# A trunk layer in split fp32: one pool's buffers change the start of all large tiles, and the third gate pass prepares its weights in another way

## Chip, core and metric

The kernel runs on one core of a Trainium2 chip. The metric is the device time of one execution in microseconds; before the change it is 1064.31 us (median of 3 runs, 1064.09 to 1064.84). Less is better.

## What is computed

One layer of a trunk on 256 tokens of width 2048: a gated linear attention mixer (4 heads, keys of 256, values of 512, chunks of 64 tokens), then a squared-ReLU MLP with 8192 hidden units, each behind an RMS norm and with a residual, and a last RMS norm.

```
proj = h @ w_in                                  # h = rmsnorm(x): q, k, v, r, g_low
log_a = log_sigmoid(g_low @ w_gate_up + b_gate) / 16
...                                              # per chunk: state = decay * state + k^T v; o = q state
o = rmsnorm(o) * o_norm
x = x + (o * silu(r)) @ w_out
a = relu(rmsnorm(x) @ w_up)
x = x + (a * a) @ w_down
```

## The kernel before

All products are in fp32 by parts. A matrix is split in a high part (a CAST on ScalarE, L1199 in the later stages) and a low part (raw minus high, on VectorE, L1205), and a product is three matmuls: high x high, high x low, low x high. A matmul has a stationary operand of 128x128 and a moving one of 128x256; 9014 of them of several stages follow each other without a break: the value pass with the gate's low rank (L149), keys and queries (L181), the scores, the second half of the values (L149), four gate passes named r, c = 0 to 3 (L669; the attention itself, L149, lies among the first), four passes of the output projection named o (L669), and then the MLP, in which up pieces (L1241) and down pieces (L1361) alternate, 48 and 42 matmuls; a tail of the down product (L149) closes it. In L1241 and L181 the weights are the stationary operand and the rows (tiles h, or x: names hh and hl, xh and xl, with h and l for high and low part) move; in L149, L669 and L1361 the rows are stationary (xh, xl, oth, otl, acts) and the weights move.

Some of the gate, o and down pieces ("summed doubles") use a scheme with 7 block products in place of 8. They need sums of weight blocks: one block is added onto another in the raw tile (rawu), then three sums are built (tile sums: L519 twice, L520), and the sums are split in turn into the tile sumshl (highs on ScalarE, L867 and L868; lows on VectorE, L520). The addition of a block onto another is an accumulating DMA issued by GpSimd (L845), except in pass c = 0 of the gate, where VectorE does it (L519, rawu<-rawu).

The order of everything outside TensorE's own sequence is a plan: each step is entered with a due time, counted in matmuls ("units") from the piece that needs it, and the steps are issued in the order of these times (at, chunk, place_chunks). For a plain double the high is due UP_HI = 75 units ahead, the low UP_LO = 56, the load UP_EARLY = 131; for a summed double 67, 50 and 165, the added block 116, the sums 68, their high parts 50 and 41, their lows 30. An engine works through its own steps in that order: SyncE issues the loads, so that a load that waits for its buffer holds up the loads behind it. rawu has three buffers in turn, and high and low three slots.

Where a tile starts in the memory of a partition follows from the pools in the order in which they are opened: const, tmp, st, turnp, later, vals and mlp lie on the left side one behind the other, the weights' slots on the right. The pool st holds seven tags of two floats; each buffer takes 32 bytes, the pool's default is four buffers per tag, and two tags (oss and ors, the attention's sums of squares and scales) ask for two. So st takes 5 x 4 x 32 + 2 x 2 x 32 = 768 bytes. The tiles behind it (xh and xl, hh and hl, the values, scores, on, oth and otl, extra, acts) start at 128 modulo 256. Tiles of rows add an offset of 48 floats (OFF), weights' slots too where the piece is an up piece or one of keys and queries. Some pieces leave the offset out: the first 24 matmuls behind each transposition, and a few others, have one operand at a multiple of 128.

Modulo 256 bytes, (start of the moving operand, start of the stationary one) is thus: value, gate and o passes (0,64); keys, queries and up (128,192); down (0,64); the pieces without offset (128,0), (0,0) or (0,128); the attention and part of the tail (128,64). Over the program these pairs form 194 stretches.

Of the kernel before, what the change touches and what calls it, by code (L numbers as in the profile page):

```python
# [27 lines left out]
F32 = mybir.dt.float32  # L28
# [4 lines left out]
P = 128  # L33
T = 256
NT = T // P
# [27 lines left out]
UP, RAWS, SUMS = 24, 24, 18  # L63
# [7 lines left out]
def tile_gla_mlp(ctx, tc, x, xt, w_vg, w_in, w_gate, w_out, w_up, w_down, final_norm, out):  # L71
# [4 lines left out]
    st = ctx.enter_context(tc.tile_pool(name="st", bufs=4))  # L76
    turnp = ctx.enter_context(tc.tile_pool(name="turnp", bufs=1))
    mixer, early = ExitStack(), ExitStack()
# [234 lines left out]
    def rsqrt(dst, ms):  # L313
        nc.gpsimd.tensor_tensor(dst, ms, mhalf, op=ALU.pow)
# [155 lines left out]
    at = later.tile([P, 2, HEADS, 3 * P + 64], F32R, tag="C", name="at")  # L470
# [147 lines left out]
    def at(time, run):  # L618
        plan.append((time, len(plan), run))

    UP_EARLY, UP_LOAD, UP_HI, UP_LO = 131, 120, 75, 56
# [6 lines left out]
    def chunk(key, hi, lo, end, load, raw):  # L628
        chunks.append((hi, len(chunks), key, lo, end, load, raw))
# [203 lines left out]
    for n, (p, c, g, summed_) in enumerate(doubles):  # L833
        key = "m", p, c, g
        time = mark(*key)
        raw = raw_u[n % 3]
        view = raw.rearrange("p (b k c) -> p b k c", b=2, k=2)
        w, c0 = (w_in, 4 * KEYW) if p == "r" else (w_out, 0)
        src = w[g * GT : (g + 1) * GT, c0 + c * GT : c0 + (c + 1) * GT].rearrange("(i p) c -> p i c", p=P)

        def load(raw=raw, src=src):
            nc.sync.dma_start(out=raw.rearrange("p (i c) -> p i c", i=4), in_=src)

        def add_block(view=view):
            nc.gpsimd.dma_start(out=view[:, :, 1, left], in_=view[:, :, 1, right], accum_op=ALU.add)  # L845

        if not summed_:
            chunk(key, time - UP_HI, time - UP_LO, time + 2 * UP, (time - UP_EARLY, load), raw)
            continue
        chunk(key, time - 67, time - 50, time + RAWS, (time - 165, load), raw)  # L850
        here = (p, c) == ("r", 0)
        if not here:
            at(time - 116, add_block)

        def adds(view=view, here=here):
            if here:
                add(view[:, :, 1, left], view[:, :, 1, left], view[:, :, 1, right])
            add(sums[:, 0], view[:, :, 1, left], view[:, :, 0, left])
            add(sums[:, 1], sums[:, 0], view[:, :, 0, right])
            sub(sums[:, 2], sums[:, 0], view[:, :, 1, right])  # L860

        def low(key=key):
            sub(sums_to[1], sums, sums_to[0].bitcast(F32))
            done.add(("sums", key))

        at(time - 68, adds)
        at(time - 50, lambda: nc.scalar.copy(sums_to[0][:, :2], sums[:, :2]))  # L867
        at(time - 41, lambda: nc.scalar.copy(sums_to[0][:, 2], sums[:, 2]))  # L868
        at(time - 30, low)


    attend_state = {}
# [12 lines left out]

    def attend_square(hd, t):
        if t == 0:
            attend_state[hd] = st.tile([P, NT], F32, tag="oss", name="oss", bufs=2)
        sq = tmp.tile([P, DV], F32, tag="t512", name="sq", bufs=3)
        nc.scalar.activation(  # L890
            sq, attend_state[hd, t], AF.Square, scale=r1k[:, t : t + 1], accum_out=attend_state[hd][:, t : t + 1]
        )

    def attend_scale(hd):
        ss = attend_state[hd]
        nc.vector.tensor_scalar(ss, ss, 1.0 / DV, EPS, op0=ALU.mult, op1=ALU.add)
        rs = attend_state[hd, "rs"] = st.tile([P, NT], F32, tag="ors", name="ors", bufs=2)
        for t in range(NT):
            rsqrt(rs[:, t : t + 1], ss[:, t : t + 1])
        nc.gpsimd.tensor_tensor(rs, rs, r1k, op=ALU.mult)  # L900
# [6 lines left out]
    for hd, t, time in attend_at:  # L907
        a = time - LENGTH
        at(a + 1, lambda hd=hd, t=t: attend_square(hd, t))
        if t:  # L910
            at(a + 14, lambda hd=hd: attend_scale(hd))
            for i in range(NT):
                at(a + 46 + 4 * i, lambda hd=hd, i=i: attend_put(hd, i))
# [223 lines left out]
    def up_time(u):  # L1137
        return 2 * UP * u if u < LEAD else cycle(u - LEAD)
# [7 lines left out]
    def plain_time(j):  # L1146
        return cycle(SUMMED - 1) + UP * j + (RAWS + SUMS if j > 1 else 0)
# [68 lines left out]
    for u in range(DOUBLES):  # L1216
        p = up_time(u)
        g, kq = divmod(u, 4)
        raw = lambda u=u: raw_d[u - 3] if u in (3, 4) else raw_u[u % 2]
# [63 lines left out]
    for g in range(GROUPS):  # L1283
# [7 lines left out]
        else:  # L1291
            c = lambda n: cycle(u - LEAD + n)
# [162 lines left out]
    for j in range(0, X_STEPS, 2):  # L1455
        p = plain_time(j)
        raw = raw_u[j // 2 % 2]
# [148 lines left out]
```

## Time and profile before

| | |
|---|---|
| time, median of 3 runs | 1064.31 us |
| the profiled execution | 1063.37 us |
| its span | 1061.3 us |
| TensorE busy | 1051.1 us, 99% |
| VectorE busy | 849.9 us, 80% |
| ScalarE busy | 690.0 us, 65% |
| GpSimd busy | 93.4 us, 9% |
| DMA, mean | 216 GB/s |

The span is the time from the first to the last instruction in the profile; the execution's time has some 2 us around it. Line numbers are those of the kernel before. A row of the costliest groups gives line, engine, operation, output and inputs by name, shape and count, then the total, the mean of one in ns, and the idle time of the engine ahead of them with what ended it. Matmuls overlap in the profile: a span of one covers its fill and its drain, so the time that one costs is the distance to the start of the next.

In the stages: the start, in which weights arrive, lasts until 57 us, keys and queries until 140, the rest of the values until 194, the gate passes until 299, the o passes until 379, up pieces alone until 436, the MLP's cycles of an up and a down piece until 998, and the tail until the end.

### The profile page before, as it was taken

To read this page: it belongs to the slowest core of one execution; us is meant where nothing else is said; L and a number is where in the kernel's file an instruction comes from. 1 tells how busy PE (TensorE), PEld (TensorE's weight loads), DVE (VectorE), ACT (ScalarE), POOL (GpSimd) and SP (SyncE) were. 2 spreads that over 40 slices of the span, in tenths; PEclk is the share of its full clock that TensorE was granted. 3 is DMA by queue.
4 is the path that set the end of the run, shared out by engine and by line. 5 is a ranking of instruction groups with operands and counts; after the bars stand their busy time and mean duration, and the time that the engine had idled before them with its cause. 6 is when DMAs were issued, how large, how long until landed. Compare 5 with 4: busy or idle time off the path is not lost.

```text
span 1061.3 us, 21237 instructions
## 1 busy us (share of the span) xinstructions
PE 1051.1 (99%) x9050; PEld 1050.7 (99%) x9050; DVE 849.9 (80%) x854; ACT 690.0 (65%) x824; POOL 93.4 (9%) x107
## 2 busy tenths in 40 slices
PE   9999999999999999999999999999999999999997
PEld 9999999999999999999999999999999999999997
DVE  7667657667686775988988988989989988989794
ACT  7675444665665754677677677676767667767752
POOL 0000000210000010101011011101011110011000
PEclk9999999999999999999999999999999999999999
DMA  9847655365766567777787878778787788787652
GB/s 341 316 155 231 197 164 164 117 207 170 278 197 220 145 234 242 224 229 228 218 230 224 231 222 244 222 211 249 217 236 220 225 229 230 213 258 214 190 198 80
DMA packets 117983, 228.74 MB, mean 216 GB/s; under 512 B 6225, under 2 KB 23121, under 8 KB 117761
## 3 DMA queue, kind: packets, MB, share of 16 engines
q1 hardware_dynamic: 99920, 208.84, 59.7%
q0 software_dynamic: 16864, 16.26, 9.8%
q10 hardware_dynamic: 1104, 2.29, 0.6%
q8 instruction: 70, 1.15, 0.4%
q14 instruction: 25, 0.20, 0.1%
HBM read 209.02 MB, written 2.10 MB: 199 GB/s over the span
## 4 chain that ended last, share of the span: by engine, by line
PE 93%; DVE 3%; ACT 1%; DMA 1%; issue 1%; POOLq 0%; POOL 0%; ACTq 0%; DVEq 0%
PE acc L1361 22%; PE acc L1241 17%; PE aux L1241 16%; PE acc L149 11%; PE acc L669 9%; PE acc L181 6%; PE aux L1361 4%; PE aux L669 2%; PE aux L181 2%; PE aux L149 2%; DVE low L1205 2%; ACT high L1199 1%; DMA rawu<-rawu 1%; DMA rawu<-in_w_in 0%; PE aux L216 0%
## 5 line engine op out<-in xcount | busy, mean ns | idle before, releaser
L1205 DVE TENSOR_TENSOR low<-rawu,high 128x2048 fp32r<-128x2048 f32 (+1 forms) x101 | 224.6, 2226 | 31.1 <-ACT high L1199 29.2
L1199 ACT CAST high<-rawu 128x2048 fp32r<-128x2048 f32 (+1 forms) x101 | 187.3, 1857 | 47.0 <-DMA rawu<-rawu 15.5
L1410 ACT CAST sumshl<-sums 128x1024 fp32r<-128x1024 f32 x112 | 88.1, 833 | 101.7 <-PE acc L1361 81.2
L1241 PE MATMUL acc<-hh,high 128*128 128x256 f32 x544 | 150.5, 277 | 0.0
L1241 PE MATMUL acc<-hh,low 128*128 128x256 f32 x544 | 150.4, 277 | 0.0
L1241 PE MATMUL acc<-hl,high 128*128 128x256 f32 x544 | 150.4, 277 | 0.0
L1205 DVE TENSOR_TENSOR low<-rawd,high 128x2048 fp32r<-128x2048 f32 (+1 forms) x59 | 132.7, 2251 | 17.8 <-ACT high L1199 17.8
L1199 ACT CAST high<-rawd 128x2048 fp32r<-128x2048 f32 (+1 forms) x59 | 110.9, 1881 | 49.2 <-PE acc L1241 39.0
L520 DVE TENSOR_TENSOR sumshl<-sums,sumshl 128x1536 fp32r<-128x1536 f32 x64 | 112.4, 1756 | 36.5 <-ACT sumshl L1410 36.1
L1241 PE MATMUL aux<-hh,high 128*128 128x256 f32 x480 | 133.2, 278 | 0.0
L1241 PE MATMUL aux<-hl,high 128*128 128x256 f32 x480 | 133.0, 277 | 0.0
L1241 PE MATMUL aux<-hh,low 128*128 128x256 f32 x480 | 133.0, 277 | 0.0
L1361 PE MATMUL acc<-high,acts 128*128 128x256 f32 x598 | 120.1, 281 | 0.0
L119 DVE TENSOR_TENSOR lo<-raw,hi 128x1024 fp32r<-128x1024 f32 (+3 forms) x68 | 78.7, 1163 | 44.7 <-ACT hi L118 44.3
L1397 POOL DMA_DIRECT2D rawd<-rawd x56 | 67.6, 1207 | 527.1 <-DVE sums L519 206.3
L118 ACT CAST hi<-raw 128x1024 fp32r<-128x1024 f32 (+3 forms) x68 | 67.7, 1001 | 56.4 <-PE acc L181 25.7
L1241 PEld LDWEIGHTS acc<-hh,high 128*128 128x128 f32 x544 | 102.2, 188 | 0.0
L1241 PEld LDWEIGHTS acc<-hh,low 128*128 128x128 f32 x544 | 102.2, 188 | 0.0
L1241 PEld LDWEIGHTS acc<-hl,high 128*128 128x128 f32 x544 | 102.2, 188 | 0.0
L1361 PE MATMUL acc<-sumshl,acts 128*128 128x256 f32 x720 | 99.4, 281 | 0.0
L1361 PEld LDWEIGHTS acc<-high,acts 128*128 128x128 f32 x598 | 98.5, 190 | 0.0
L1361 PEld LDWEIGHTS acc<-sumshl,acts 128*128 128x128 f32 x720 | 91.1, 189 | 0.0
(346 smaller groups left out, 2802.5 us busy)
## 6 DMA issues: line engine op xcount, KB each, us to landing
rawu<-in_w_up SPq DMA_DIRECT2D x124, 512.0 KB, 4.5
rawd<-in_w_down SPq DMA_DIRECT2D x56, 1024.0 KB, 5.2
raw<-in_w_in SPq DMA_DIRECT2D x48, 512.0 KB, 4.6
rawu<-in_w_in SPq DMA_DIRECT2D x16, 1024.0 KB, 5.1
rawu<-in_w_out SPq DMA_DIRECT2D x16, 1024.0 KB, 5.7
rawd<-rawd POOLq DMA_DIRECT2D x56, 256.0 KB, 5.4
rawu<-in_w_down SPq DMA_DIRECT2D x16, 512.0 KB, 4.5
raw<-in_w_vg SPq DMA_DIRECT2D x13, 520.0 KB, 8.6
```

The lines of the kernel that those rows point to most:

```text
L118: last_hi[0] = nc.scalar.copy(hi[:, s], raw[:, s])
L119: last_lo[0] = nc.vector.tensor_tensor(lo[:, s], raw[:, s], hi[:, s].bitcast(F32), op=ALU.subtract)
L149: nc.tensor.matmul(o[:, m], x, w[:, m], start=first and c == 0, stop=last, skip_group_check=True)
L181: nc.tensor.matmul(o, u[:, s], m[:, kt], start=kt == 0 and n == 0 and j % 2 == 0, stop=kt == KT - 1 and n == 2, skip_group_check=True,)
L520: sub = lambda o, x, y: nc.vector.tensor_tensor(o, x, y, op=ALU.subtract)
L669: nc.tensor.matmul(b[:, o], a[x], w[y], start=(pc, name) in fresh, stop=last and i == 2, skip_group_check=True)
L1199: nc.scalar.copy(o, i)
L1205: nc.vector.tensor_tensor(o, i, x.bitcast(F32), op=ALU.subtract)
L1241: nc.tensor.matmul(o, w[:, s], row_h(kt)[m], start=kt == 0 and n == 0 and j % 2 == 0, stop=kt == KT - 1 and n == 2, skip_group_check=True,)
L1361: nc.tensor.matmul(bank[:, o], a[x], w[y], start=fresh and i == 0, stop=d + 1 in starts + [SUMMED] and i == 2, skip_group_check=True,)
L1397: nc.gpsimd.dma_start(out=view[:, :, 1, left], in_=view[:, :, 1, right], accum_op=ALU.add)
L1410: nc.scalar.copy(sums_to[0][:, f], sums[:, f])
```

## The change

The change has three parts.

1. The tags oss and ors take the pool's four buffers in place of two. The pool st grows from 768 to 896 bytes, and each tile behind it on the left side starts 128 bytes later. The right side, and h and the tiles before st, do not move. The pairs become (0,192) in all passes, pieces and the tail, 8576 matmuls, (0,0) in the pieces without offset, 240, and (0,128) for the sums of x, 96; besides there are the small and the transposing ones. 59 stretches are left, the last of them 5172 matmuls at (0,192); the 24 at (0,0) ahead of it belong to the early down and up pieces. The sequence of TensorE's instructions is the same.
2. In the third gate pass (r, c = 2) VectorE adds the blocks of both summed doubles, as in the first; the two accumulating DMAs of L845 for them are gone.
3. In the gate passes c = 1 to 3, the highs and lows are due 14 units sooner for plain doubles and 13 for summed ones; loads 42 units sooner for plain doubles and 13 for summed; the sums 26 units sooner.

```
-            chunk(key, time - UP_HI, time - UP_LO, time + 2 * UP, (time - UP_EARLY, load), raw)
+            early = 14 if here and c else 0
+            chunk(key, time - UP_HI - early, time - UP_LO - early, time + 2 * UP, (time - UP_EARLY - 3 * early, load), raw)
             continue
-        chunk(key, time - 67, time - 50, time + RAWS, (time - 165, load), raw)
-        here = (p, c) == ("r", 0)
+        early = 13 if here and c else 0
+        chunk(key, time - 67 - early, time - 50 - early, time + RAWS, (time - 165 - early, load), raw)
...
-        at(time - 68, adds)
+        at(time - 68 - 2 * early, adds)
...
-            attend_state[hd] = st.tile([P, NT], F32, tag="oss", name="oss", bufs=2)
+            attend_state[hd] = st.tile([P, NT], F32, tag="oss", name="oss")
...
-        rs = attend_state[hd, "rs"] = st.tile([P, NT], F32, tag="ors", name="ors", bufs=2)
+        rs = attend_state[hd, "rs"] = st.tile([P, NT], F32, tag="ors", name="ors")
```

Ahead of the first of these lines stands here = p == "r", which is true for all four gate passes where it was true for the first alone. Behind L847 the lines of the changed kernel are 2 higher.

On VectorE, at the third gate pass (low is the low part of a weight tile, rawu the raw one, sums the sums of blocks, extra a copy of rows, on the attention's output), there stood before:

```order
L984 TENSOR_TENSOR on<-on,sr 128x512
L1205 TENSOR_TENSOR low_2344<-rawu_2346,high_2343 128x2048
L1205 TENSOR_TENSOR low_2350<-rawu_2347,high_2349 128x2048
L1016 CAST extra<-xl 128x512
L1205 TENSOR_TENSOR low_2352<-rawu_2348,high_2351 128x2048
L519 TENSOR_TENSOR sums<-rawu_2346 128x512
L519 TENSOR_TENSOR sums<-sums,rawu_2346 128x512
L520 TENSOR_TENSOR sums<-sums,rawu_2346 128x512
L1205 TENSOR_TENSOR low_2344<-rawu_2346,high_2343 128x2048
```

and now, at the same place:

```order
L986 TENSOR_TENSOR on<-on,sr 128x512
L1207 TENSOR_TENSOR low_2344<-rawu_2346,high_2343 128x2048
L1207 TENSOR_TENSOR low_2350<-rawu_2347,high_2349 128x2048
L1207 TENSOR_TENSOR low_2352<-rawu_2348,high_2351 128x2048
L1018 CAST extra<-xl 128x512
L519 TENSOR_TENSOR rawu_2346<-rawu_2346 128x2x256
L519 TENSOR_TENSOR sums<-rawu_2346 128x512
L519 TENSOR_TENSOR sums<-sums,rawu_2346 128x512
L520 TENSOR_TENSOR sums<-sums,rawu_2346 128x512
L1207 TENSOR_TENSOR low_2344<-rawu_2346,high_2343 128x2048
```

The block is added on VectorE ahead of the sums, and a low has moved ahead of the copy of rows; the second summed double of the pass gets its add in the same way.

SyncE's loads at the end of the gate passes (in_w_in and in_w_out are the weights of gate and o, in_x the residual's rows) stood before:

```order
L842 DMA rawu_2347<-in_w_in 128x4x512
L842 DMA rawu_2348<-in_w_in 128x4x512
L1072 DMA h<-in_x 128x1024 x2
L842 DMA rawu_2346<-in_w_in 128x4x512
L1072 DMA h<-in_x 128x1024 x2
L842 DMA rawu_2347<-in_w_out 128x4x512
```

and now:

```order
L842 DMA rawu_2347<-in_w_in 128x4x512
L842 DMA rawu_2348<-in_w_in 128x4x512
L842 DMA rawu_2346<-in_w_in 128x4x512
L1074 DMA h<-in_x 128x1024 x4
L842 DMA rawu_2347<-in_w_out 128x4x512
```

The last load of gate weights has moved ahead of the residual's four.

More of the change, by code (lines that the diff above doesn't have):

```diff
@@ L845, in add_block @@
             nc.gpsimd.dma_start(out=view[:, :, 1, left], in_=view[:, :, 1, right], accum_op=ALU.add)
+        here = p == "r"
         if not summed_:
-            chunk(key, time - UP_HI, time - UP_LO, time + 2 * UP, (time - UP_EARLY, load), raw)
+            early = 14 if here and c else 0
+            chunk(key, time - UP_HI - early, time - UP_LO - early, time + 2 * UP, (time - UP_EARLY - 3 * early, load), raw)
             continue
-        chunk(key, time - 67, time - 50, time + RAWS, (time - 165, load), raw)
-        here = (p, c) == ("r", 0)
+        early = 13 if here and c else 0
+        chunk(key, time - 67 - early, time - 50 - early, time + RAWS, (time - 165 - early, load), raw)
         if not here:
```

## The prediction

> **What bounds the kernel now.** I read the page first: busy shares, then the chain that ended last.
>
> ```profile
> span 1061.3 us, 21237 instructions
> PE 1051.1 (99%) x9050; PEld 1050.7 (99%) x9050; DVE 849.9 (80%) x854; ACT 690.0 (65%) x824; POOL 93.4 (9%) x107
> PE 93%; DVE 3%; ACT 1%; DMA 1%; issue 1%; POOLq 0%; POOL 0%; ACTq 0%; DVEq 0%
> ```
>
> TensorE has no gaps to speak of and is 93% of the chain, so time can come only from two things: how far apart its matmuls start, and its few stalls. The costliest groups give a first hint: the same shape costs 277 ns at L1241 (up) and 281 ns at L1361 (down).
>
> ```profile
> L1241 PE MATMUL acc<-hh,high 128*128 128x256 f32 x544 | 150.5, 277 | 0.0
> L1361 PE MATMUL acc<-high,acts 128*128 128x256 f32 x598 | 120.1, 281 | 0.0
> ```
>
> These spans overlap, so I went to the windows: stretches inside one stage, with the count of matmuls. A count includes those still running at the left edge, so the distance from start to start is (window + 0.28 us) / count, 0.28 being the span of one. Read column 2 (the window's length) and the first (x...).
>
> ```profile
> core 0: us, PE busy (x) PEld busy (x) DVE busy (x) ACT busy (x) POOL busy (x), PEclk, DMA share, GB/s
> 78.00:139.90 61.90, 61.90 (x549) 61.90 (x548) 44.01 (x76) 30.73 (x36) 2.33 (x16) 1.00 0.67 205
> 140.20:151.00 10.80, 10.80 (x94) 10.80 (x93) 5.78 (x9) 5.01 (x9) 0.00 (x0) 1.00 0.67 196
> 160.30:194.20 33.90, 33.90 (x290) 33.90 (x290) 21.57 (x28) 15.21 (x17) 0.00 (x0) 1.00 0.47 156
> 194.30:220.70 26.40, 26.40 (x228) 26.40 (x227) 17.11 (x17) 19.45 (x30) 7.52 (x9) 1.00 0.42 127
> 299.20:345.70 46.50, 46.50 (x397) 46.50 (x396) 35.79 (x31) 26.40 (x28) 2.42 (x2) 1.00 0.66 197
> 350.80:378.90 28.10, 28.10 (x250) 28.10 (x249) 23.34 (x21) 18.84 (x26) 1.20 (x1) 1.00 0.50 154
> 379.00:384.50 5.50, 5.50 (x49) 5.50 (x49) 4.85 (x6) 1.90 (x1) 0.00 (x0) 1.00 1.05 401
> 406.30:435.90 29.60, 29.60 (x264) 29.60 (x263) 21.57 (x21) 18.07 (x18) 2.43 (x2) 1.00 0.74 229
> 436.00:998.00 562.00, 562.00 (x4858) 562.00 (x4857) 500.28 (x416) 395.52 (x432) 65.17 (x54) 1.00 0.78 228
> 462.00:467.40 5.40, 5.40 (x50) 5.40 (x49) 5.40 (x4) 3.35 (x4) 0.00 (x0) 1.00 0.59 168
> 467.50:472.40 4.90, 4.90 (x44) 4.90 (x43) 4.80 (x7) 2.37 (x2) 1.22 (x1) 1.00 0.95 281
> 999.00:1053.00 54.00, 54.00 (x461) 54.00 (x460) 42.16 (x59) 30.25 (x46) 0.57 (x1) 1.00 0.45 156
> ```
>
> There are two paces and little between. Key and query (78 on): 62.18/549 = 113.3 ns. The value pass (160.3): 34.18/290 = 117.9 ns. PEclk is 1.00 in both, so it is not the clock; nor is it the operation, since one line (L669) runs 46.78/397 = 117.8 ns from 299.2 and 28.38/250 = 113.5 ns from 350.8, with the same two engines and less DMA in the second but not in 406.3, also fast (29.88/264 = 113.2) at DMA share 0.74. In the MLP the pace alternates: 462.0 is one up piece (L1241), 5.68/50 = 113.6; 467.5 one down piece (L1361), 5.18/44 = 117.7.
>
> What changes where the pace changes is where the operands start. Write (moving, stationary) for the start addresses modulo 256 bytes as the pools lay them out: up is (128,192), down (0,64), the value and gate passes and the o projection (0,64), key and query (128,192). At 139.9 the pair goes from (128,192) to (0,64), fast to slow; at 378.9 from (0,64) to (128,192), fast to slow; in the MLP every move up to down goes fast to slow and back. So a pair is not fast or slow by itself: a move of both operands by 128 bytes flips a pace that otherwise stays (549 matmuls, 397, 264 without a switch). One move disagrees: at 51.2 us (0,64), slow, is followed by (128,192), slow too, 4.88/41 = 119 ns (the last row of the next fence). A second kind of place resets it: 24 matmuls with the stationary operand at 0 or 128.
>
> **The change part by part.** *Memory.* Dropping bufs=2 on two tags gives each the pool's 4 buffers of 32 bytes: 2 x 2 x 32 = 128 bytes more, and every left-side tile after that pool moves from 128 to 0 modulo 256. Then up, down, value, gate, o and tail all are (0,192): 194 stretches of constant pair become 59, and the last 5172 matmuls (nearly all the MLP and the tail) have no switch. By the flips above, nothing would flip there any more. Which pace they keep is decided by the reset ahead of them, 24 matmuls at (0,0) and then (0,192). In this trace six resets go from a stationary operand at 0 to one at 192 with the moving operand unmoved (they end at 59.9, 77.3, 389.2, 406.1, 443.8 and 454.3 us), and all six end fast (386.5 below is one, followed by 389.4: 13.58/120 = 113.2); but their moving operand is at 128. The one reset at (0,0), 157.5 below, goes to 64, and ends slow (the 160.3 row). Of three resets at (0,128) going to 64, one ends fast (350.8) and two slow (257.6, 299.2). I take fast: the move of the stationary operand, 0 to 192, is the one that ended fast each time.
>
> ```profile
> 157.50:160.10 2.60, 2.60 (x23) 2.60 (x23) 2.54 (x7) 1.05 (x5) 0.00 (x0) 1.00 0.00 0
> 386.50:389.10 2.60, 2.60 (x24) 2.60 (x24) 2.34 (x7) 2.39 (x7) 0.00 (x0) 1.00 1.05 400
> 257.70:261.00 3.30, 3.30 (x30) 3.30 (x29) 2.63 (x3) 2.75 (x4) 0.00 (x0) 1.00 0.80 243
> 389.40:402.70 13.30, 13.30 (x120) 13.30 (x119) 8.89 (x10) 7.62 (x12) 3.02 (x3) 1.00 0.04 14
> 51.40:56.00 4.60, 4.60 (x41) 4.60 (x40) 4.25 (x8) 3.86 (x11) 0.00 (x0) 1.00 0.72 238
> ```
>
> Each window's gain is its time less count x 113.3 ns. MLP: 562.28 - 550.41 = 11.9, less 0.3 for two resets that stay, 11.6. Tail from 999: 54.28 - 52.23 = 2.0. 299.2: 46.78 - 44.98 = 1.8. 160.3: 34.18 - 32.86 = 1.3. 140.2: 11.08 - 10.65 = 0.4. 379.0: 0.2. 194.3: 26.68 - 25.83 = 0.85, of which I take 0.6, since the sums of x, stationary, stay at 128. 257.7: 3.58 - 3.40 = 0.2. Sum 18.1. Resets at (0,0) cost 2.88/23 = 125 ns against 2.88/24 = 120 at (128,0), the first with the stall of a transposition in it; for 10 resets I book 0.3, between 0 and 10 x 24 x 5 ns = 1.2.
>
> The Trainium skill, "SBUF — State Buffer", section "Who interferes with whom", says that TensorE has two independent read ports, one for the moving operand and one for weights, and never waits on anyone. By that the address would not matter, and this term would be 0, not 18.1. The trace does not agree: L669's 117.8 and 113.5 ns stand with equal clock and operations.
>
> *Third gate pass.* The chain between 230 and 300 us holds the only long stall of TensorE.
>
> ```profile
> 236.31 7.28 DMA rawu<-rawu
> 243.74 1.93 ACT high L1199
> 245.69 2.29 DVE low L1205
> ...
> 275.86 2.30 DVE low L1205
> 278.21 11.73 PE acc L669 x101
> ```
>
> ```profile
> ACT high L1199 <- DMA rawu<-rawu: 9.3, 1, 9.3
> DVE sums L519 <- DMA rawu<-rawu: 7.4, 1, 7.4
> PEld acc L669 <- DVE low L1205: 1.9, 1, 1.9
> PE acc L669 <- DVE low L1205: 1.7, 1, 1.7
> ```
>
> ```profile
> L519 DVE TENSOR_TENSOR rawu<-rawu x2: 682/684/686, 192.2 to 202.3; 128x512 f32<-128x512 f32 x2
> L845 POOL DMA_DIRECT2D rawu<-rawu x2: 1207/1278/1350, 236.3 to 242.9; - x2
> ```
>
> The accumulating DMA takes 7.28 us; ACT waits 9.3 us and DVE 7.4 us for it, DVE then runs without a break from 243.7 to 278, and its last low is 1.7 to 1.9 us late for TensorE. The change puts two 0.684 us adds on DVE, ahead of the sums, in time in which it idled 7.4 us, and takes both DMAs and 2 x 1.3 us of GpSimd away: 1.37 us into 7.4 us idle, so nothing on the path. *Sooner.* Thirteen or fourteen units (one is a matmul, 0.115 us) put highs and lows 1.5 to 1.6 us, plain loads 42 units or 4.8 us, and sums 3 us earlier. With both, the late low has 7.4 - 1.4 + 1.5 = 7.5 us more against 1.9 needed: -1.8 us. Behind a high that comes sooner, ACT holds up the squares and puts of the attends (one high: 1.93 us); behind a load that comes sooner, SP's queue holds the loads of x into h, which are not wanted before the o projection. Bounds for new waits: 0, and 1.9 us, the stall that this trace shows for such a slip; I take 0.4, near none, since TensorE waits here once only. Below nothing is excluded, as this cannot speed TensorE past its pace.
>
> Sum against the profiled execution, 1063.37 us: -18.1 + 0.3 - 1.8 + 0.4 = 1044.2. The median shown is 0.94 above it: 1045.1, so **1045 us**. The case spans 1042 (no new wait, no cost of the resets, and 0.2 ns less for each of 8576 matmuls, 1.7 us) to 1049 (each bound at its worse end, 0.9 and 1.5 us, and two of the smaller stages that stay slow, 1.8 us).
>
> **The rivals.** *The one pace is the slow one (slower).* Place: the resets at (0,0), above all the last, ahead of the 5172. If they leave TensorE slow, as at 160.3, all that is now fast slows to 117.8 ns. MLP: 4858 x 0.1178 = 572.3, +10.0; 78.0: 64.67 - 62.18 = +2.5; 350.8, 389.4 and 406.3: +1.1, +0.6, +1.2; and the three rows below +1.1, +0.4 and +0.6.
>
> ```profile
> 221.00:248.70 27.70, 27.70 (x247) 27.70 (x246) 17.90 (x20) 16.30 (x19) 3.89 (x5) 1.00 0.67 199
> 265.50:276.00 10.50, 10.50 (x95) 10.50 (x94) 7.33 (x12) 5.85 (x7) 0.00 (x0) 1.00 0.79 280
> 278.50:294.40 15.90, 15.90 (x142) 15.90 (x142) 9.54 (x6) 8.00 (x7) 0.00 (x0) 1.00 0.68 223
> ```
>
> Together +17.5: 1064.3 + 17.5 - 1.8 + 0.3 = 1080. If only the last reset fails, the MLP costs 10.0 more, the tail stays as it is, and the other stages still gain 18.1 - 11.6 - 2.0 = 4.5: 1064.3 + 10.0 - 4.5 - 1.5 = 1068. For it: the only (0,0) reset seen ended slow. Against: six of six with the same move of the stationary operand. It decides at one point, whether L1241 and L1361 are both at 281 ns. 0.15.
>
> *Fast only in part.* A faster TensorE asks more of VectorE: 500.28 us busy of 562 becomes 500.28 of 550.4, 91%, and lows that came just in time come late; or one of the early resets fails while the last holds. Each low late by the 1.9 us seen, two to six of them, or 117.8 ns kept in the value and o stages (4.5 us): 1049 to 1060. For it: DVE is 89% busy in the MLP already. Against: no wait of TensorE in the MLP now. 0.11.
>
> *The address does not set the pace.* The Trainium skill's sentence above is that case. Worked from the rows: the pace stays as it is and only the stall goes: 1064.3 - 1.8 = 1062.5. Against it: every switch of the pace falls on a switch of the pair. 0.04.
>
> **How the numbers follow.** Forecast 0.70, slow 0.15, in part 0.11, address idle 0.04. The range takes the forecast with its bounds and the partial case, 0.81 together: 1042 to 1060. A measurement of this kernel can tell about 0.2%, 2 us, from no change, so 1062.5 counts as no change: faster 0.81, same 0.04, slower 0.15.
>
> **What would show it.** Right: L1361's matmuls at 277 ns as L1241's; windows in the MLP with about 4960 matmuls in 562 us; the value pass at 113.3; no wait of TensorE for a low near 276 us; POOL two DMAs fewer. Wrong: 281 ns at both lines, or L1241 and L1361 still apart; new rows of PE waiting for low in the MLP.

## The result, and the profile after

The changed kernel takes 1046.04 us (median of 5 runs, 1045.96 to 1048.25) where the kernel before takes 1064.11 (5 runs) beside it: a ratio of 0.9834, with a 95% interval of 0.982 to 0.9848. The profiled execution takes 1046.55 us, its span 1044.7; before they were 1063.37 and 1061.3. The forecast was 1045 us.

The page of the changed kernel begins, in the same order as that of before:

```profile
span 1044.7 us, 21232 instructions
PE 1036.4 (99%) x9050; PEld 1036.2 (99%) x9050; DVE 850.8 (81%) x856; ACT 689.7 (66%) x824; POOL 92.5 (9%) x105
PE 98%; issue 1%; ACT 0%; DVE 0%; POOLq 0%; POOL 0%; ACTq 0%
```

TensorE now is 98% of the chain instead of 93%, and the share of every other engine rounds to 0%. The two rows by which the hint was found, up and down, after the change (line, engine, operation, count, then busy time and mean ns of one):

```profile
L1243 PE MATMUL acc<-hh,high 128*128 128x256 f32 x544 | 150.6, 277 | 0.0
L1363 PE MATMUL acc<-high,acts 128*128 128x256 f32 x598 | 116.0, 276 | 0.0
```

Down fell from 281 to 276 ns; up stayed at 277. The windows, which are to be read as before, (window + 0.28 us) / count:

```profile
160.30:194.20 33.90, 33.90 (x301) 33.90 (x300) 22.48 (x29) 16.48 (x18) 0.00 (x0) 1.00 0.47 156
221.00:248.70 27.70, 27.70 (x238) 27.70 (x237) 20.50 (x21) 16.12 (x15) 1.26 (x3) 1.00 0.55 190
257.80:260.90 3.10, 3.10 (x30) 3.10 (x29) 3.10 (x2) 0.00 (x0) 0.00 (x0) 1.00 0.12 46
265.50:293.40 27.90, 27.90 (x239) 27.90 (x238) 19.56 (x19) 14.62 (x15) 0.00 (x0) 1.00 0.69 236
299.20:342.70 43.50, 43.50 (x386) 43.50 (x385) 34.87 (x30) 25.47 (x26) 2.56 (x2) 1.00 0.68 206
436.00:998.00 562.00, 562.00 (x4959) 562.00 (x4958) 509.77 (x426) 404.48 (x444) 65.19 (x54) 1.00 0.79 231
999.00:1037.00 38.00, 38.00 (x338) 38.00 (x337) 30.03 (x49) 18.56 (x32) 0.57 (x1) 1.00 0.43 151
```

The MLP runs 4959 matmuls in the 562 us that held 4858, 562.28/4959 = 113.4 ns; the values (34.18/301 = 113.6), the o projection (43.78/386 = 113.4) and the tail (38.28/338 = 113.3) are fast too. VectorE is busy 509.77 of 562 us and TensorE does not wait for it. But two windows are slow: the second gate pass (221.0: 27.98/238 = 117.6), which was fast before, and the fourth (265.5: 28.18/239 = 117.9), also fast before. The waits of TensorE that were there near 276 us are gone: the only one left in the whole program is the first.

```profile
PE aux L216 <- DVE square L213: 1.1, 1, 1.1
```

### The profile page after: what moved, and what is told of

It is laid out like the page before. It is cut to its first block, busy times and chain, and to the rows that moved or that the text cites. A ratio compares the mean times of both kernels' runs of the same rounds, so it can differ in the third digit from the quotient of the medians.

```text
span 1044.7 us, 21232 instructions
## 1 busy us (share of the span) xinstructions
PE 1036.4 (99%) x9050; PEld 1036.2 (99%) x9050; DVE 850.8 (81%) x856; ACT 689.7 (66%) x824; POOL 92.5 (9%) x105
## 4 chain that ended last, share of the span: by engine, by line
PE 98%; issue 1%; ACT 0%; DVE 0%; POOLq 0%; POOL 0%; ACTq 0%
PE acc L1363 21%; PE acc L1243 18%; PE aux L1243 16%; PE acc L669 12%; PE acc L149 11%; PE acc L181 6%; PE aux L669 4%; PE aux L1363 4%; PE aux L181 2%; PE aux L149 2%; PE aux L216 0%; PE acc L739 0%; PE acc L479 0%; PE aux L479 0%; ACT sqf L1497 0%
## 5 line engine op out<-in xcount | busy, mean ns | idle before, releaser
L1363 PE MATMUL acc<-high,acts 128*128 128x256 f32 x598 | 116.0, 276 | 0.0
L118 ACT CAST hi<-raw 128x1024 fp32r<-128x1024 f32 (+3 forms) x68 | 67.7, 1001 | 56.0 <-PE acc L181 25.7
L1363 PE MATMUL acc<-sumshl,acts 128*128 128x256 f32 x720 | 96.0, 276 | 0.0
L1243 PEld LDWEIGHTS aux<-hh,high 128*128 128x128 f32 x480 | 90.2, 188 | 0.0
```

The lines of the kernel that those rows point to most:

```text
L118: last_hi[0] = nc.scalar.copy(hi[:, s], raw[:, s])
L1243: nc.tensor.matmul(o, w[:, s], row_h(kt)[m], start=kt == 0 and n == 0 and j % 2 == 0, stop=kt == KT - 1 and n == 2, skip_group_check=True,)
L1363: nc.tensor.matmul(bank[:, o], a[x], w[y], start=fresh and i == 0, stop=d + 1 in starts + [SUMMED] and i == 2, skip_group_check=True,)
```

## The experiments

**The two halves of the change apart.** The first moves the same tiles by the same 128 bytes without touching the buffers of oss and ors.

```
     ms1 = st.tile([P, NT], F32, name="ms1")
+    st.tile([P, NT], F32, name="spare")          # kernel before, else unchanged
```

> The kernel before with one spare tile of 4 buffers x 32 bytes in the pool st: all left-side tiles move by 128 bytes, oss and ors keep two buffers, the gate passes are prepared as before. Theory (the start addresses set the pace): the pairs are those of the changed kernel, so L1361 runs at 276 ns as L1241 does, and the time falls by all but the 1.8 us of the stall: 1046.5 to 1048. Rival (two more buffers for oss and ors are what helps, by waits that go): nothing changes, 1064.

Measured 1048.27 us, ratio 0.985 (0.9837 to 0.9864). The pace of the MLP is that of the changed kernel, 562.28/4959, and the late low of the gate is still there:

```profile
437.00:999.00 562.00, 562.00 (x4959) 562.00 (x4958) 509.37 (x425) 404.17 (x444) 65.18 (x54) 1.00 0.79 230
```

```profile
PEld acc L670 <- DVE low L1206: 1.8, 2, 1.5
PE acc L670 <- DVE low L1206: 1.3, 1, 1.3
```

So 128 bytes of unused memory carry nearly the whole gain, and more buffers for oss and ors are not needed for it. Outside the start and the gate passes the traces of e1 and of the changed kernel gain the same, stage by stage, within 0.01 us. What the other half adds on top of the new addresses is not clear of the spread: the changed kernel's ratio is 0.9834, and 0.9849 where it was measured again (e11). The other half alone, with the old addresses:

```
-            attend_state[hd] = st.tile([P, NT], F32, tag="oss", name="oss")
+            attend_state[hd] = st.tile([P, NT], F32, tag="oss", name="oss", bufs=2)   # kernel after; ors alike
```

> The second and third part of the change alone, oss and ors with two buffers, so that all addresses are those of before. Theory: the stall near 276 us goes and nothing else, 1064.1 - 1.9 = 1062.2, and L1361 stays at 281 ns. Rival (the sooner steps are what frees TensorE elsewhere too): under 1060. Rival (the adds on VectorE or the loads ahead of x bring a new wait): 1064 or more.

Measured 1063.15 us, ratio 0.9991 (0.9982 to 1.0): the stall is down from 1.9 to 0.2 us, but the time fell by only 0.6.

```profile
PEld acc L669 <- DVE low L1207: 0.2, 1, 0.2
```

The profile says where the rest went. Before, the second gate pass ran 247 matmuls from 221.0 to 248.7; here, with the same addresses and no stall in that window, the first row has 237:

```profile
221.00:248.70 27.70, 27.70 (x237) 27.70 (x236) 20.40 (x22) 16.98 (x17) 1.26 (x3) 1.00 0.57 191
278.20:293.40 15.20, 15.20 (x137) 15.20 (x136) 8.86 (x6) 7.94 (x7) 0.00 (x0) 1.00 0.70 235
```

The pass is slow, 10 matmuls short, 1.06 us. In the starts of before there is a small pause of TensorE at 220.8 us, 133 ns from start to start where its neighbours have 118, and behind it the pace is 113 ns:

```profile
220.84 0.29 PE L669 MATMUL aux<-high,xh 128*128 128x256 f32 x1
220.98 0.28 PE L669 MATMUL aux<-low,xh 128*128 128x256 f32 x1
```

Here the pause is missing and the pace stays at 118. So a pause may bring the fast pace; no run sets one on purpose.

The two edits of this half apart:

```
-        here = (p, c) == ("r", 0)
+        here = p == "r"                                # e3: kernel before, nothing sooner
```

> The kernel before with the block addition of the third gate pass on VectorE alone; nothing is due sooner, addresses as before. Theory: the accumulating DMA was what ACT and DVE waited 9.3 and 7.4 us for, so this alone takes away the stall of 1.9 us: 1062.2. Rival (being sooner is what takes it away): the low near 276 us is still late, 1063.5 to 1064.1.

```
         early = 13 if here and c else 0
+        here = (p, c) == ("r", 0)                      # e4: as e2, the accumulating DMA kept
```

> The kernel before with highs, lows, loads and sums of the later gate passes sooner, the accumulating DMA kept. Theory: the DMA is still waited for, and the sums, now 26 units sooner in VectorE's order, hold the lows behind them up: the stall stays or grows, 1063.5 to 1068. Rival (sooner is what counts): the stall goes, 1062.2.

The block addition alone gives 1062.55 us, ratio 0.9986 (0.9977 to 0.9995), with no wait for a low left; the sooner steps alone 1063.08, ratio 0.999 (0.9982 to 0.9999), with one of 0.2 us. My expectation for the second failed: being sooner by itself takes nearly all of the stall away, though VectorE still waits for the DMA. Either half of the edit would have done nearly all of it. Both kernels lose the same 1.06 us in the second pass, where the pause is missing again; in e3 the same two matmuls are 0.11 us apart:

```profile
221.39 0.28 PE L669 MATMUL aux<-high,xh 128*128 128x256 f32 x1
221.50 0.28 PE L669 MATMUL aux<-low,xh 128*128 128x256 f32 x1
```

In e3 nothing is due sooner, and up to this point every engine runs the same instructions in the same order as before. Being sooner is therefore not what takes the pause away. The pause is there in the traces of before and of e1 (217 ns at 220.3 us), and in no trace of a kernel whose gate passes were edited. With one trace of each kernel, whether the edit or chance decides on it stays open. In e4 the 313 ns gap that is left at 277.2 us is followed by the slow pace, in e2 one of 312 ns at 277.1 by the fast one (15.48/137 = 113.0 in the window above):

```profile
278.20:293.40 15.20, 15.20 (x131) 15.20 (x130) 8.47 (x6) 7.99 (x7) 0.00 (x0) 1.00 0.64 212
```

**Does the reset decide?** Four up pieces leave the offset out for half of their 48 matmuls; here they keep it.

```
-    SAME = (1, 4, LEAD + 1, LEAD + 2)
+    SAME = ()
```

> The changed kernel with the offset kept in the four up pieces that leave it out: the four stretches of 24 matmuls at (0,0) in the up and early MLP stages become (0,192), the resets elsewhere stay. Theory (a reset decides the pace and it then stays): after the transposition near 382 us nothing brings TensorE back, so some 5760 matmuls run at 117.8 ns: +25.9, less 0.6 for the resets saved, 1071. Rival (one pair everywhere is enough, a transposition does not matter): 1045.4.

Measured 1071.73 us, ratio 1.0073 (1.0056 to 1.009). TensorE is slow from the transposition at 384 us to the end, with the same pair everywhere; in the MLP 562.28/4774 = 117.8:

```profile
455.00:1017.00 562.00, 562.00 (x4774) 562.00 (x4774) 492.86 (x411) 391.59 (x429) 62.77 (x52) 1.00 0.77 222
```

So one pair everywhere does not make TensorE fast. It only keeps what it has. The four stretches of 24 matmuls at (0,0), each of which costs 0.16 us more than it would at the fast pace, make the difference of 25.7 us. The mechanism of my slower rival is real, and what kept the changed kernel from it is the direction in which the operand leaves the reset:

```
-OFF = 48
-WRAP = 16
+OFF = 16
+WRAP = 48
```

> The changed kernel with an offset of 16 floats in place of 48 everywhere (and 48 for the wrapped columns of keys and queries): one pair everywhere as well, but (0,64) in place of (0,192); the resets at (0,0) are as many. Theory (a reset from 0 to 64 leaves the slow pace, as at 160.3 us of before, one from 0 to 192 the fast one): nearly all matmuls at 117.8 ns, +33: 1079. Rival (one pair everywhere, whichever, is fast): 1043 to 1046.

Measured 1079.76 us, ratio 1.0152 (1.0137 to 1.0167). No stage is fast; up and down both have 281 ns. The same resets at (0,0), left to 64 instead of 192, leave the slow pace each time. The pair (0,64) is not slow by itself: the down pieces of e8, below, have it and run at the fast pace. The rows of up and down in e7:

```profile
L1243 PE MATMUL acc<-hh,high 128*128 128x256 f32 x544 | 153.0, 281 | 0.0
L1363 PE MATMUL acc<-high,acts 128*128 128x256 f32 x598 | 120.0, 281 | 0.0
```

**Which operand flips it?** Once the stationary operand alone changes between up and down, by 128 bytes, and once the moving one alone.

```
-        places = [a[:, KT * T + OFF : KT * T + OFF + n] for a in turned_h]
-        places += [most[:, OFF + i * n : OFF + (i + 1) * n] for i in range(10)]
+        places = [a[:, KT * T + 16 : KT * T + 16 + n] for a in turned_h]
+        places += [most[:, 16 + i * n : 16 + (i + 1) * n] for i in range(10)]      # e8
```

> The changed kernel with the activations (stationary in the down pieces) 128 bytes earlier: up (0,192), down (0,64), so that the stationary operand alone changes its start at each switch in the MLP; memory and order are otherwise as changed. Theory (any switch of the pair may flip the pace): the down pieces and parts of the up pieces are slow again, L1363 at 281 ns, 1057 or more. Rival (only a move of both operands flips it): 1046.

```
-        return [a[:, kt * T : (kt + 1) * T] for a in turned_h]
+        return [a[:, 32 + kt * T : 32 + (kt + 1) * T] for a in turned_h]           # e9
```

> The changed kernel with the rows of tile h 128 bytes later: up (128,192), down and tail (0,192), so that in the MLP the moving operand alone changes its start at each switch. Theory (the moving operand's half of 256 bytes, not the stationary one's, is what flips the pace): down pieces at 281 ns again, up pieces at 277, 1057.5. Rival (only a move of both operands flips it): 1046.

Measured: e8 1046.97 us, ratio 0.9844 (0.9829 to 0.9858); e9 1058.87, ratio 0.9956 (0.9942 to 0.997). The window that held 4961 matmuls in the changed kernel, first for e8, then for e9:

```profile
455.00:1017.00 562.00, 562.00 (x4961) 562.00 (x4961) 508.94 (x436) 403.64 (x444) 62.76 (x52) 1.00 0.79 230
```

```profile
455.00:1017.00 562.00, 562.00 (x4865) 562.00 (x4864) 499.74 (x422) 400.07 (x440) 62.78 (x52) 1.00 0.77 225
```

In e8 nothing flips: (0,64) and (0,192) alternate, all fast. In e9 up is at 276 ns and down at 279, close to the 277 and 281 of before the change:

```profile
L1243 PE MATMUL acc<-hh,high 128*128 128x256 f32 x544 | 150.4, 276 | 0.0
L1363 PE MATMUL acc<-high,acts 128*128 128x256 f32 x598 | 119.9, 279 | 0.0
```

Of my two expectations for e8 the rival's number held, though not its reason, that only a move of both operands flips the pace: in the MLP a change of the stationary operand by 128 bytes does not flip it, and a change of the moving one does. This narrows the prediction's rule, which spoke of a move of both.

It is still not a rule for every switch. In the kernel before, at the end of the tail, the moving operand alone goes back and forth between (0,64) and (128,64), at least eight times, and the pace stays slow, 13.68/116 = 117.9:

```profile
1040.20:1053.60 13.40, 13.40 (x116) 13.40 (x114) 4.78 (x13) 3.70 (x10) 0.57 (x1) 1.00 0.20 78
```

There the stationary operand is at 64, in e9 at 192. No run tests whether that is the reason.

**What is left.** In the changed kernel the sums of x (tile h, at 192) are at (0,128), and behind them the gate passes are slow.

```
-    const.tile([P, 16], F32, name="pad")
+    const.tile([P, 32], F32, name="pad")
...
     r1k = const.tile([P, NT], F32, name="r1k")
+    const.tile([P, 48], F32, name="pad2")
...
-        oth, otl = (vals.tile([P, KT * T + 128], F32R, tag="B", name="ot" + i) for i in "hl")
+        oth, otl = (vals.tile([P, KT * T + 64], F32R, tag="B", name="ot" + i) for i in "hl")
```

> The changed kernel with tile h at 0 modulo 256 too (64 bytes more ahead of it, 192 behind it, 64 floats less in oth and otl, which they do not use), so that the sums of x are (0,192) instead of (0,128). Theory (the stretches at (0,128) throw the first, second and third gate pass off the fast pace): those passes run at 113.3 ns, -0.7 - 1.0 - 1.2 and -0.5 for the 96 matmuls themselves: 1042.6. Rival (the attention's pieces or the raw sums throw it off): 1046.

Measured 1044.83 us, ratio 0.9823 (0.9809 to 0.9838), 2.2 us more than expected. From 160.6 to 250.9 us there is one pace, 90.58/799 = 113.4, and against the trace of the changed kernel the first two gate passes gain 2.05 us; the later ones gain 0.1 where 1.2 was expected for the third. The faster passes brought a late low back, and behind it the pace is lost (the second row: 16.68/142 = 117.5):

```profile
160.60:250.90 90.30, 90.30 (x799) 90.30 (x799) 65.61 (x71) 55.04 (x66) 10.35 (x12) 1.00 0.52 173
275.00:291.40 16.40, 16.40 (x142) 16.40 (x141) 9.66 (x6) 8.00 (x7) 0.00 (x0) 1.00 0.63 209
```

The timeline shows the matmul that starts 0.55 us behind the one ahead of it, and the starts on either side, 0.11 and 0.12 us apart:

```profile
273.86 0.28 PE L670 MATMUL acc<-high,xl 128*128 128x256 f32 x1
273.97 0.28 PE L670 MATMUL acc<-high,xh 128*128 128x256 f32 x1
274.52 0.39 PE L670 MATMUL acc<-low,xh 128*128 128x256 f32 x1 [0.27 <-DVE low L1208]
274.75 0.28 PE L670 MATMUL acc<-high,xl 128*128 128x256 f32 x1
274.87 0.28 PE L670 MATMUL acc<-high,xh 128*128 128x256 f32 x1
```

The last version builds on this one: it takes that low 8 units sooner and leaves two resets out.

```
-    ... time - UP_LO - early, time + 2 * UP, ...
+    ... time - UP_LO - early - (8 if early and (c, g) == (3, 2) else 0), time + 2 * UP, ...
...
-    SAME = (1, 4, LEAD + 1, LEAD + 2)
+    SAME = (1, 4)
```

> The kernel with h at 0 modulo 256, the low of the fourth gate pass that was 0.55 us late there 8 units sooner, ahead of the second product with the gate, and two of the four stretches without offset of the up pieces (those in the MLP's first cycles) left out. Theory: the late low goes (-0.4), the 144 matmuls behind it keep 113.3 ns (-0.65), the two resets save 48 x 6.7 ns (-0.3): 1044.8 - 1.4 = 1043.4. Rival (a reset in the MLP is needed): over 1050. Rival (the low is late anyway): 1044.5.

> The changed kernel once more, beside the other two on one chip: 1046.0.

Measured, beside each other: 1043.21 us, ratio 0.9813 (0.9799 to 0.9826), and the changed kernel again 1047.28, ratio 0.9849 (0.9836 to 0.9863), where 1046.0 was expected. The low is no longer waited for, and the resets in the MLP's first cycles were not needed: between the last reset that stays and the place where they were, nothing changes the moving operand's start. The profiled execution of this version lost 1 us in the tail, where a gap of 280 ns near 1014.0 us ended the fast pace (19.48/166 = 117.3 behind it):

```profile
1000.00:1013.80 13.80, 13.80 (x124) 13.80 (x123) 10.65 (x15) 6.50 (x8) 0.00 (x0) 1.00 0.60 193
1014.80:1034.00 19.20, 19.20 (x166) 19.20 (x165) 13.45 (x24) 7.69 (x20) 0.57 (x1) 1.00 0.19 73
```

The waits put the gap down to VectorE: the first weight load of a piece that writes aux waits 0.2 us while VectorE still adds what stands there to h.

```profile
PEld aux L149 <- DVE h L520: 0.2, 1, 0.2
```

## Why the prediction was right, and where a step was not

The table sets the steps of the forecast beside what the stages gained, measured from the first matmul of a stage to that of the next in the two profiled executions. The sum is that of the unrounded numbers.

| step | forecast, us | measured, us |
|---|---|---|
| MLP | -11.6 | -11.4 |
| tail | -2.0 | -2.1 |
| o passes | -1.8 | -1.8 |
| values | -1.3 - 0.4 | -1.3 - 0.4 |
| up pieces ahead of the MLP, with 0.3 for resets | -0.2 + 0.3 | -0.2 |
| gate passes, with the stall and 0.4 for new waits | -0.6 - 0.2 - 1.8 + 0.4 | +0.1 |
| start | 0 | +0.7 |
| sum | -19.2 | -16.3 |

The profiled execution is 2.4 us above the 1044.2 worked out for it. That the median is only 1 us above the 1045 is partly luck: the profiled execution of before lay 0.9 us below its median, that of the changed kernel 0.5 above.

*The pace.* Right, in sign and size: e1 shows it alone, and e5, e7, e8 and e9 test its links. The place on which I put the slower rival, the reset ahead of the last 5172 matmuls, was the right one. That the operand leaves it for 192 and not for 64 decided for 18 us less instead of 16 more (e7). I had argued this from six cases with another moving operand, and it held.

*The flip.* "A move of both operands by 128 bytes flips a pace" was too wide: in the MLP the moving operand alone does it (e9), the stationary one alone not (e8). It was also too general: besides the exception that the prediction names, at 51.2 us, the moves in the tail of before flip nothing. Why is not known. The number did not depend on it: in the changed kernel the moving operand starts at 0 in all the passes, the MLP and the tail.

*The read ports.* The Trainium skill, "SBUF — State Buffer", section "Who interferes with whom", gives TensorE two independent read ports and says that it never waits on anyone. That is about one engine holding up another. The prediction read from it that the address would not matter, which is more than it says; the runs neither contradict it nor follow from it. With equal matmuls, clock and data, e7 and the changed kernel differ by 33 us through the starts of tiles alone.

*The stall.* It went, as forecast. The step that failed is the one beside it: the sum took the pace of the gate passes to be independent of the gate edit, and left the second pass out as fast already. That pass had been fast behind the small pause at 220.8 us, which no view that I had quoted showed, and which also breaks the prediction's statement that every switch of the pace falls on a switch of the pair. Without the pause it is slow (e2, e3, e4: +1.06 us each, without any change of address). In the changed kernel the passes behind the sums of x are slow: 0.0, +1.1 and -0.9 us in the first, the second and the last two, where I had booked -0.6, 0 and -2.0. Of the 1.8 us of the stall, the slow pace behind it took back about half. e6 shows what keeps the first two slow there, the stretches at (0,128): with h moved, they gain 2.05 us.

*New waits.* The 0.4 us were not needed: no wait for a low is left. VectorE at 91% does not hold TensorE up; that rival did not come about.

*The start.* I had booked nothing for it, and part of the 0.7 us belongs to the change. From matmul 100 to matmul 404 of the program the four traces with the old addresses (before, e2, e3, e4) take 36.2 us each, and the eight in which these matmuls are at (0,192) take 36.5 each. The stage is slow in both, and slower with the new addresses: 36.28/305 = 119.0 ns before, 36.28/302 = 120.1 after (the first and second row). The rest lies in the first 15 us, while weights arrive, in which traces of kernels with equal addresses differ by up to 0.7 us.

```profile
15.00:51.00 36.00, 36.00 (x305) 36.00 (x304) 24.48 (x32) 24.85 (x34) 1.08 (x2) 1.00 0.94 338
15.40:51.40 36.00, 36.00 (x302) 36.00 (x302) 23.41 (x30) 23.83 (x32) 1.08 (x2) 1.00 0.94 330
```

What decides the pace after a pause stays open. Measured from start to start, pauses of 133 and 217 ns (before at 220.8 us, e1 at 220.3) were followed by the fast pace in place of the slow one, and pauses of 280, 319 and 550 ns (e10; e1 at 247.6; e6) by the slow one in place of the fast. The 1.97 us of before left the fast pace as it was and the 1.58 us of e1 the slow one; 312 ns in e2 left the fast pace, 313 ns in e4 ended it.

## What to carry to other kernels

Where a kernel is bound by TensorE, divide stretches of the profile by their matmuls before looking for waits: a difference of 4.5 ns that no wait shows was worth 17 us here, nine times the only long stall. Keep the start of the moving operand modulo 256 bytes equal through the program, and look at the pace behind each transposition, since here 24 matmuls at another start decided whether it came back (e5); a few bytes more in an early pool can move every tile behind it. A stall may cost more than its length if the pace behind it is the slower one.

## What the runs showed of the hardware

- Matmuls of 128x128 by 128x256 in fp32 parts start 113.3 or 117.8 ns apart at the same granted clock (0.998 to 0.999), and either lasts for thousands of matmuls: 5172 at (0,192) were all fast in the changed kernel, all slow in e5. In the first stage, in which weights arrive, the distance is 119 ns before and 120 after.
- In the MLP a change of the moving operand's start by 128 bytes flips the pace at each switch, with the stationary operand at 192 (e9); one of the stationary operand by 128 does not (e8: 4961 matmuls in 562 us). In the tail of before, with the stationary operand at 64, changes of the moving one flip nothing (117.9 ns throughout).
- 24 matmuls with both starts at 0 modulo 256 run at 120 ns. Going on with the stationary operand at 192 they leave the fast pace, at 64 the slow one, in every case of these runs. That is what the traces show; the reason is not known.
- Behind a short pause of TensorE, 0.13 to 0.55 us from start to start, the pace was faster than ahead of it in two cases, slower in four, and the same in one. No run sets a pause on purpose.
